# Low halves of the weights all on VectorE, the first norm's affine in half tiles, and new step lengths around the layer-B softmax

## The chip, the cores and the metric

The program runs on one core of a Trainium2 chip. The metric is the device time of one execution in microseconds, from the first instruction to the last. The time shown is the median of three executions. A profile is one more execution, recorded on the chip, with a time of its own.

## The reference, cut to what matters

Two blocks run one after the other, each on 256 tokens (two tiles of 128). The first is a pooling mixer (layer A), a layer norm, and a mixer with dilated window attention (layer B); the second is two attention layers with their MLPs (layer0, mlp0, layer1, mlp1). The change touches the first norm and layer B's attention directly, and the weights of layer B's end, layer0, mlp0's first part and layer1.

```python
def layer_norm(x, g, b):
    mu = jnp.mean(xf, axis=-1, keepdims=True)
    var = jnp.mean(jnp.square(xf - mu), axis=-1, keepdims=True)
    y = (xf - mu) * lax.rsqrt(var + LN_EPS) * g + b
...
for l in range(DEPTH):
    if l < N_A_LAYERS: y = pool_mixer(h, ...)        # layer A
    else:              y = dilated_mixer(h, w_in_b, w_out_b, k_sh, v_sh, slopes)  # layer B
    h = layer_norm(DN_ALPHA * h + y, ln_g[l], ln_b[l])
    if l == N_A_LAYERS - 1:
        kv = h @ w_kv          # keys and values of layer B
...
# dilated_window_attention, per head and dilation:
scores = jnp.einsum('bnqrhd,bnkrhd->bnrhqk', qb, kk) * (HEAD_DIM ** -0.5)
p = jnp.exp(scores + bias - lse[..., None])
out = jnp.einsum('bnrhqk,bnkrhd->bnqrhd', p, vv)
```

All of it is float32. Every product with a weight matrix `h @ w` is the bulk of the work.

## The kernel before, in words

**Products.** A float32 product is made of three reduced-precision ones (`mm3`): high part by high part (L189), high by low (L190), low by high (L191), all summed in PSUM. So each weight block is loaded by `stream` as a tile `ws` of 128x1024, ScalarE (ACT) casts it to the high part `wh` (L130), and the low part `wl = ws - wh` is made either by VectorE (DVE) in one instruction of 128x1024 (L138) or by GpSimd (POOL) in two of 128x512 (L136). The string `self.lo` decides: its letters are walked through load by load, D is DVE and P is POOL. It is "D" in layers A and B and "DP" or "DDP" in stretches of layer0, mlp0 and layer1, so that 31 of 336 loads go to POOL. There are five buffers each of `wh` and `wl`. Activations are split in the same way (`split`: L143 on ACT, L144 on DVE).

**Order.** TensorE (PE) runs its instructions in the order in which the code is written. The work of the side generators is woven into the projections: `tick(us)` advances a clock by the estimated length of the projection step just written, adds `us * ratio` to a budget, and calls `step` until the budget is spent; each `yield x` of a generator takes x from it. The other engines are ordered by a scheduler, which also takes `issue_after(i)` (it keeps an instruction behind i) and `high_priority` into account. Every engine then runs its own list in order and waits for semaphores of the others.

**The first norm.** `out_norm` calls `layer_norm` for each tile t of tokens: sum with the residual (L548) and statistics (L549) on DVE, `rstd`, whose power runs on POOL (L177, priority raised), normalization on DVE (L557, two halves of 512 columns), then the affine n*g+b with rows of g and b that are broadcast to all partitions (L498, POOL, 128x1024, a product and a sum for each tile). The transposed copy that feeds layer B doesn't need the affine in that form: `norm_T` transposes n on PE (L385) and applies g and b per partition while evacuating PSUM (L410 on DVE), then splits into high and low (L143, L144). The L498 result is used as residual after layer B.

**Attention of layer B.** `attn1` is one generator for each of eight head pairs, woven into the projections of the following head pair. For each of two query tiles (qt) it makes scores for two heads on PE (L668), adds the distance bias (L672, DVE), takes the row maximum (L673, DVE) and the exponential (L674, ACT), and yields. Then 1/sum (L678) and the scaling (L680) on DVE, four groups of transposes of the weights on PE (L690, evacuated by L691), and products with the values (L703). L276 are small PE products for a modulation vector, put between.

**Norms of the second block** follow the same pattern: L1075 and L1078 (residual with gate), L174 and L177 (rstd), L720 (normalization), L385 (transposes). L750, L756 and L758 are the rotary embedding (L756 on POOL).

Of the kernel before, what the change touches and what calls it, by code (L numbers as in the profile page):

```python
# [8 lines left out]
F32 = mybir.dt.float32  # L9
F32R = mybir.dt.float32r  # L10
AF = mybir.ActivationFunctionType
ALU = mybir.AluOpType
# [51 lines left out]
class Kern:  # L64
    def __init__(self, tc, I, out):
        self.tc, self.nc, self.I, self.out = tc, tc.nc, I, out
        self.clock = 0.0
        self.due = []
        self.sides = []
        self.budget = 0.0  # L70
        self.ratio = 0.0
        self.marks = set()
        self.mupto = 99
        self.nload = 0
        self.lo = "D"
# [47 lines left out]
    def stream(self, src):  # L123
        nc = self.nc
        k, c = src.shape[1], src.shape[2]
        n = k * c
        ws = self.wp.tile([128, 1024], F32, name="ws", tag="ws", bufs=4)
        nc.sync.dma_start(ws[:, :n].rearrange("p (k c) -> p k c", k=k), src)
        wh = self.wp.tile([128, 1024], F32R, name="wh", tag="wh", bufs=5)
        nc.scalar.copy(wh[:, :n], ws[:, :n])  # L130
        wl = self.wp.tile([128, 1024], F32R, name="wl", tag="wl", bufs=5)
        self.nload += 1
        if self.lo[self.nload % len(self.lo)] == "P":
            for i in range(0, n, 512):
                c = slice(i, i + 512)
                nc.gpsimd.tensor_tensor(wl[:, c], ws[:, c], wh[:, c].bitcast(F32), op=ALU.subtract)  # L136
        else:
            nc.vector.tensor_sub(wl[:, :n], ws[:, :n], wh[:, :n].bitcast(F32))  # L138
        return (wh[:, :n].rearrange("p (k c) -> p k c", k=k),
                wl[:, :n].rearrange("p (k c) -> p k c", k=k))  # L140
# [291 lines left out]
    def layer_a(self):  # L432
        nc, I = self.nc, self.I
# [10 lines left out]
        with self.tc.tile_pool(name="pa", bufs=1) as pa:  # L444
# [9 lines left out]
            n = 0  # L454
# [40 lines left out]
        with self.tc.issue_after(pw.ins):  # L495
            for n in ns:
                for z, op in ((self.lng[0], ALU.mult), (self.lng[1], ALU.add)):
                    nc.gpsimd.tensor_tensor(n, n, z, op=op)  # L498
# [81 lines left out]
    def layer_b(self):  # L580
# [5 lines left out]
        for cb in range(6):  # L586
# [18 lines left out]
            if cb == 3:  # L605
                with self.tc.issue_after(i0.ins), self.tc.issue_after(i1.ins):
                    self.tables()
        wq = I["w_in_b"][0]
        mg = self.fms(4, F32)
        with self.tc.tile_pool(name="pb", bufs=2) as pb:  # L610
# [3 lines left out]
            for hp in range(8):  # L614
# [20 lines left out]
                self.weave(self.attn1(hp, kq[1], kq[0], vt, mg[hp // 2][:, (hp % 2) * 256:(hp % 2) * 256 + 256]), 0.58)  # L635
# [18 lines left out]
    def attn1(self, hp, q, k, vt, mg):  # L654

        nc = self.nc
        sbs = [self.pb.tile([128, 2, 512], F32, name="sb") for _ in range(2)]
        st = [[self.sm(2) for _ in range(3)] for _ in range(2)]
        for qt in range(2):
# [15 lines left out]
            yield 2.0  # L675
# [5 lines left out]
        yield 0.8  # L681
        pts = []
        for r in range(2):
            pt = [self.fm(F32) for _ in range(2)]
            for i in range(2):
                ps = self.ps("B")
                for b in range(2):
                    for qt in range(2):
                        c, d = (i * 2 + b) * 128, (b * 2 + qt) * 128
                        nc.tensor.transpose(ps[:, d:d + 128], sbs[r][:, qt, c:c + 128], self.ident)  # L690
                (nc.scalar.copy if i else nc.vector.tensor_copy)(pt[i], ps)  # L691
                yield 0.5
            pts.append([pt[i // 2][:, (i % 2) * 256:(i % 2) * 256 + 256] for i in range(4)])
            yield 1.2
# [5 lines left out]
        for n, (g, b, kt, Q) in enumerate(todo):  # L700
# [4 lines left out]
            if n % 2:  # L705
                yield 0.8
# [397 lines left out]
    def layer0(self):  # L1104
        nc, I = self.nc, self.I
        self.X[1] = [(x[:, 0:512], x[:, 512:1024]) for x in self.xt]
        self.lo = "DP"
# [68 lines left out]
        self.lo = "DP"  # L1176
        self.in_block(0, acts, 0, 512, (0, 1), fin_qa)
        self.lo = "D"
# [17 lines left out]
        self.lo = "DP"  # L1196
        wv = self.in_block(0, acts, 1792, 512, (0,), fin_vb)
        self.lo = "DDP"
# [6 lines left out]
        self.lo = "DDP"  # L1205
        self.out_cols(0, osl, 0, fill)
        self.lo = "DP"
# [55 lines left out]
    def mlp0(self):  # L1263
        nc, I = self.nc, self.I
        joint = self.j1
        self.lo = "DP"
# [8 lines left out]
        for c in range(4):  # L1275
            hh, hl = self.hidden(0, c, act, 512, first if c == 0 else None)
            if c == 0:
                self.lo = "D"
# [65 lines left out]
    def mlp1(self):  # L1344
        nc, I = self.nc, self.I
        act = self.act1
        self.lo = "D"
# [51 lines left out]
    def layer1(self):  # L1399
        nc, I = self.nc, self.I  # L1400
        acts = {s: self.act256(*self.hs1[s]) for s in (0, 1)}
        self.lo = "DP"
# [154 lines left out]
```

## Time and profile before

| what | value |
|---|---|
| time, median of 3 (lowest, highest) | 1553.2 us (1547.85, 1554.77) |
| profiled execution, its own time | 1556.21 us |
| span of the profile | 1554.4 us |
| busy PE, DVE, ACT, POOL | 1481.7, 920.0, 722.8, 248.7 us |
| mean granted clock of PE | 0.983 |

The span is 1.8 us shorter than the profiled execution's time, and this execution lies 3 us above the median. An engine that is busy for 95% of the span can only be made to end earlier by closing its gaps or by letting it run at full clock; the rows below list gaps with the engine and instruction that ended them.

### The profile page before, as it was taken

How to read it: one execution, taken by the hardware profiler on the slowest of the kernel's cores; microseconds unless marked ns; L12 is line 12 of the kernel's file. 1: busy time of each engine (PE TensorE's matmuls, PEld its weight loads, DVE VectorE, ACT ScalarE, POOL GpSimd, SP SyncE). 2: the span in 40 equal slices, each digit the busy share in tenths (PEclk: the TensorE clock that was granted, in tenths of full speed). 3: DMA queues.
4: the chain of work that ended last, by engine and by line, in shares of the span. 5: the costliest groups of instructions: out<-in, count | busy, mean ns of one | idle time of the engine just before them, and what ended most of it. 6: DMA issues, size and time to landing. Idle time of an engine off the chain costs nothing. (4 is left out here: it accounts for less than half of the span.)

```text
span 1554.4 us, 23369 instructions
## 1 busy us (share of the span) xinstructions
PE 1481.7 (95%) x8966; PEld 1224.9 (79%) x8966; DVE 920.0 (59%) x1629; ACT 722.8 (46%) x1397; POOL 248.7 (16%) x298
## 2 busy tenths in 40 slices
PE   8999899999999899999879999999998999999998
PEld 8898578887999687776668777777886886689987
DVE  5676855556667867457685233343448687565554
ACT  4454444444455545556564232231326476454443
POOL 4431200001010342113330000000014423100000
PEclk9999899999999999999999999999999999999999
DMA  8567576766464723013333444443353345645652
GB/s 279 188 195 262 166 225 184 230 188 211 130 199 150 245 94 94 30 55 122 120 110 120 151 149 136 149 137 121 95 161 97 109 97 202 229 138 190 189 183 89
DMA packets 186544, 241.80 MB, mean 156 GB/s; under 512 B 15296, under 2 KB 132080, under 8 KB 186368
## 3 DMA queue, kind: packets, MB, share of 16 engines
q1 hardware_dynamic: 185168, 237.11, 48.2%
q0 software_dynamic: 1264, 3.19, 0.6%
q8 instruction: 70, 1.15, 0.3%
q14 instruction: 42, 0.34, 0.1%
HBM read 239.19 MB, written 2.03 MB: 155 GB/s over the span
## 5 line engine op out<-in xcount | busy, mean ns | idle before, releaser
L138 DVE TENSOR_TENSOR wl<-ws,wh 128x1024 fp32r<-128x1024 f32 x305 | 377.9, 1240 | 360.3 <-ACT wh L130 351.0
L130 ACT CAST wh<-ws 128x1024 fp32r<-128x1024 f32 x336 | 351.0, 1048 | 401.3 <-PE ps L191 205.6
L189 PE MATMUL ps<-fm,wh 128*128 128x256 f32 (+1 forms) x1416 | 432.8, 306 | 4.5 <-ACT fm L143 4.4
L191 PE MATMUL ps<-fm,wl 128*128 128x256 f32 (+1 forms) x1416 | 426.0, 301 | 7.5 <-DVE wl L138 7.5
L190 PE MATMUL ps<-fm,wh 128*128 128x256 f32 (+1 forms) x1416 | 425.4, 300 | 0.3 <-DVE fm L144 0.3
L189 PE MATMUL ps<-wh,fm 128*128 128x512 f32 (+1 forms) x912 | 364.7, 400 | 0.0
L190 PE MATMUL ps<-wl,fm 128*128 128x512 f32 (+1 forms) x912 | 356.0, 390 | 6.3 <-DVE wl L138 6.3
L191 PE MATMUL ps<-wh,fm 128*128 128x512 f32 (+1 forms) x912 | 356.1, 390 | 2.7 <-DVE fm L144 2.7
L189 PEld LDWEIGHTS ps<-fm,wh 128*128 128x128 f32 x1416 | 271.5, 192 | 30.0 <-issue 7.1
L191 PEld LDWEIGHTS ps<-fm,wl 128*128 128x128 f32 x1416 | 271.8, 192 | 18.4 <-DVE wl L138 9.2
L190 PEld LDWEIGHTS ps<-fm,wh 128*128 128x128 f32 x1416 | 272.2, 192 | 9.6 <-DVE fm L144 0.7
L189 PEld LDWEIGHTS ps<-wh,fm 128*128 128x128 f32 x912 | 173.4, 190 | 58.4 <-issue 18.5
L191 PEld LDWEIGHTS ps<-wh,fm 128*128 128x128 f32 x912 | 172.9, 190 | 43.7 <-DVE fm L144 5.2
L190 PEld LDWEIGHTS ps<-wl,fm 128*128 128x128 f32 x912 | 173.5, 190 | 42.9 <-DVE wl L138 8.1
L136 POOL TENSOR_TENSOR wl<-ws,wh 128x512 fp32r<-128x512 f32 x62 | 87.9, 1437 | 498.3 <-ACT wh L130 444.1
L143 ACT CAST fm<-t 128x128 fp32r<-128x128 f32 (+2 forms) x232 | 85.0, 393 | 137.7 <-POOL t L474 51.5
L144 DVE TENSOR_TENSOR fm<-t,fm 128x128 fp32r<-128x128 f32 (+2 forms) x232 | 95.0, 434 | 57.8 <-ACT fm L143 56.8
L177 POOL TENSOR_TENSOR sm<-sm,mhalf 128x1 f32<-128x1 f32 (+3 forms) x42 | 37.2, 885 | 393.7 <-DVE sm L174 298.2
L926 ACT ACTIVATE e<-ps,sm 128x512 f32<-128x512 f32 (+1 forms) x96 | 59.3, 618 | 50.0 <-DVE sm L922 34.8
L922 DVE TENSOR_REDUCE sm<-ps 128x1 f32<-128x512 f32 (+1 forms) x96 | 56.1, 589 | 12.8 <-PE ps L1041 9.2
L870 POOL CAST fm<-fm 64x256 fp32r<-64x256 f32 x32 | 18.0, 563 | 231.0 <-ACT fm L867 218.2
L1340 DVE SCALAR_TENSOR_TENSOR t<-ps,t 128x512 f32<-128x512 f32 (+1 forms) x64 | 35.4, 552 | 18.5 <-ACT t L1339 18.5
(204 smaller groups left out, 1287.6 us busy)
## 6 DMA issues: line engine op xcount, KB each, us to landing
ws<-in_w_mlp_in_dram SPq DMA_DIRECT2D x64, 512.0 KB, 3.8
ws<-in_w_mlp_out_dram SPq DMA_DIRECT2D x64, 512.0 KB, 3.8
mw<-in_w_mod_dram SPq DMA_DIRECT2D x48, 512.0 KB, 4.9
fm<-in_w_mod_dram SPq DMA_DIRECT2D x96, 256.0 KB, 5.4
ws<-in_w_kv_dram SPq DMA_DIRECT2D x48, 512.0 KB, 3.9
ws<-in_w_in_dram SPq DMA_DIRECT2D x40, 512.0 KB, 4.0
ws<-in_w_in_a_dram SPq DMA_DIRECT2D x32, 512.0 KB, 5.0
ws<-in_w_in_b_dram SPq DMA_DIRECT2D x32, 512.0 KB, 4.0
```

The costliest lines, as they stand in the source:

```text
L130: nc.scalar.copy(wh[:, :n], ws[:, :n])
L136: nc.gpsimd.tensor_tensor(wl[:, c], ws[:, c], wh[:, c].bitcast(F32), op=ALU.subtract)
L138: nc.vector.tensor_sub(wl[:, :n], ws[:, :n], wh[:, :n].bitcast(F32))
L143: self.nc.scalar.copy(hi, src)
L144: self.nc.vector.tensor_sub(lo, src, hi.bitcast(F32))
L177: self.pow = nc.gpsimd.tensor_tensor(r, v, self.mhalf[:, :n], op=ALU.pow)
L189: nc.tensor.matmul(ps, a[0], b[0], start=start, stop=False)
L190: nc.tensor.matmul(ps, a[0], b[1], start=False, stop=False)
L191: nc.tensor.matmul(ps, a[1], b[0], start=False, stop=stop)
L922: nc.vector.tensor_reduce(nm, ps[:, :n], axis=AX.X, op=ALU.max, negate=True)
L926: nc.scalar.activation(e, ps[:, :n], AF.Exp, bias=nm, accum_out=ss)
L1340: nc.vector.scalar_tensor_tensor(q, p, 0.0, r, op0=ALU.max, op1=ALU.mult)
```

## The change

The low parts made by POOL are made by DVE; the pattern string, its counter and the L136 branch are gone. The affine of the first norm leaves `out_norm`; it becomes a list of eight half-tile instructions, of which two each are issued after the evacuation of a value block (cb = 1 to 4) in layer B, with `issue_after` on that block's two evacuations. In `attn1` the ratio goes from 0.58 to 0.66 and the lengths of the yields change.

```diff
@@ stream
-        self.nload += 1
-        if self.lo[self.nload % len(self.lo)] == "P":
-            for i in range(0, n, 512):
-                c = slice(i, i + 512)
-                nc.gpsimd.tensor_tensor(wl[:, c], ws[:, c], wh[:, c].bitcast(F32), op=ALU.subtract)
-        else:
-            nc.vector.tensor_sub(wl[:, :n], ws[:, :n], wh[:, :n].bitcast(F32))
+        nc.vector.tensor_sub(wl[:, :n], ws[:, :n], wh[:, :n].bitcast(F32))
@@ end of layer A
-        with self.tc.issue_after(pw.ins):
-            for n in ns:
-                for z, op in ((self.lng[0], ALU.mult), (self.lng[1], ALU.add)):
-                    nc.gpsimd.tensor_tensor(n, n, z, op=op)
+        self.affine = [(n[:, c:c + 512], z[:, c:c + 512], op) for n in ns for c in (0, 512)
+                       for z, op in ((self.lng[0], ALU.mult), (self.lng[1], ALU.add))]
@@ layer_b, after i0 and i1 of value block cb
+            if cb:
+                with self.tc.issue_after(i0.ins), self.tc.issue_after(i1.ins):
+                    for _ in range(2):
+                        if self.affine:
+                            n, z, op = self.affine.pop(0)
+                            nc.gpsimd.tensor_tensor(n, n, z, op=op)
@@ attn1
-                self.weave(self.attn1(hp, kq[1], kq[0], vt, mg[hp // 2][:, (hp % 2) * 256:(hp % 2) * 256 + 256]), 0.58)
+                self.weave(self.attn1(hp, kq[1], kq[0], vt, mg[hp // 2][:, (hp % 2) * 256:(hp % 2) * 256 + 256]), 0.66)
-            yield 2.0
+            yield (1.5, 3.2)[qt]
...
-        yield 0.8
+        yield 1.2
...
-                yield 0.5
+                yield 0.4
...
-            yield 1.2
+            yield 0.6
...
-                yield 0.8
+                yield 0.6
@@ layer0, the first of the lines that set self.lo
-        self.lo = "DP"
...
```

Three places show how the instructions stand before and after. In the program after, lines have other numbers: L138 of before is L130, L144 is L136, L177 is L169, L498 is L604, L668 is L665, L690 is L687, L276 is L268, L189 is L181, L174 is L166, L720 is L717, L1075 and L1078 are L1072 and L1075.

POOL, from the end of layer A into layer B, before:

```order
70 L613 DMA dist<-in_dist_dram 128x1024
71 L177 TENSOR_TENSOR sm<-sm,mhalf 128x1 x2
72 L498 TENSOR_TENSOR xt<-xt,gb 128x1024 x4
73 L804 TENSOR_TENSOR t_2547<-t_2545 128x128
74 L870 COPY fm<-fm 64x256 x24
```

and after:

```order
70 L610 DMA dist<-in_dist_dram 128x1024
71 L169 TENSOR_TENSOR sm<-sm,mhalf 128x1
72 L604 TENSOR_TENSOR xt<-xt,gb 128x512 x4
73 L169 TENSOR_TENSOR sm<-sm,mhalf 128x1
74 L604 TENSOR_TENSOR xt<-xt,gb 128x512 x4
75 L801 TENSOR_TENSOR t_2547<-t_2545 128x128
```

The first tile's four affine instructions stand ahead of the power (L169) of the second tile's rstd, where before both powers stood ahead of all of them; `issue_after` names instructions of DVE and ACT, and in POOL's list no instruction of layer B stands ahead of them.

PE, head pair 1 of layer B, before (three matmuls L189, L190, L191 repeat eight times in each gap of 24 rows, shown as "..."; a gap of 48 rows holds sixteen such threes):

```order
1775 L668 MATMUL ps<-fm 128x128 x4
...
1801 L668 MATMUL ps<-fm 128x128 x4
1802 L276 MATMUL ps<-mw,S 32x512 x4
...
1827 L690 MATMUL ps<-ident,sb 128x128 x4
...
1852 L690 MATMUL ps<-ident,sb 128x128 x4
1853 L276 MATMUL ps<-mw,S 32x512 x4
1854 L690 MATMUL ps<-ident,sb 128x128 x4
...
1879 L690 MATMUL ps<-ident,sb 128x128 x4
```

and after:

```order
1774 L665 MATMUL ps<-fm 128x128 x4
1775 L874 MATMUL ps<-fm 128x256 x4
1776 L665 MATMUL ps<-fm 128x128 x4
...
1801 L268 MATMUL ps<-mw,S 32x512 x4
...
1850 L687 MATMUL ps<-ident,sb 128x128 x12
1851 L268 MATMUL ps<-mw,S 32x512 x4
1852 L687 MATMUL ps<-ident,sb 128x128 x4
```

The scores of both query tiles now stand back to back. Between the last scores and the first transposes lay one group of 24 matmuls and an L276; now there are three groups and an L268, and the transposes follow one another where a group of 24 stood between them.

DVE, the first norm of mlp0 (xt is a token tile, t_8584 and t_8576 its normalized form), before:

```order
827 L174 TENSOR_SCALAR sm<-sm 128x1
828 L1078 SCALAR_TENSOR_TENSOR xt<-t_8571,sm,xt 128x512
829 L1078 SCALAR_TENSOR_TENSOR xt<-t_8572,sm,xt 128x512
830 L138 TENSOR_TENSOR wl<-ws,wh 128x1024
831 L174 TENSOR_SCALAR sm<-sm 128x1
832 L720 TENSOR_SCALAR t_8584<-xt,sm 128x512 x2
```

and after:

```order
844 L166 TENSOR_SCALAR sm<-sm 128x1
845 L130 TENSOR_TENSOR wl<-ws,wh 128x1024
846 L1075 SCALAR_TENSOR_TENSOR xt<-t_8563,sm,xt 128x512
847 L1075 SCALAR_TENSOR_TENSOR xt<-t_8564,sm,xt 128x512
848 L130 TENSOR_TENSOR wl<-ws,wh 128x1024 x2
849 L166 TENSOR_SCALAR sm<-sm 128x1
850 L130 TENSOR_TENSOR wl<-ws,wh 128x1024
851 L717 TENSOR_SCALAR t_8576<-xt,sm 128x512 x2
```

Four low parts (L130) stand between the first L166 and the normalization (L717), where one (L138) stood.

## Rows read from the trace of the kernel before

**Rows 1.** Page, part 1: busy time, share of the span and instructions of each engine.
```profile
PE 1481.7 (95%) x8966; PEld 1224.9 (79%) x8966; DVE 920.0 (59%) x1629; ACT 722.8 (46%) x1397; POOL 248.7 (16%) x298
```

**Rows 2.** Waits of PE: total us, times, longest.
```profile
PE ps L385 <- DVE t L720: 12.5, 6, 4.1
...
PE ps L690 <- DVE sb L680: 6.2, 4, 1.9
```

**Rows 3.** Windows (columns us, busy us of each engine, granted clock, DMA share, GB/s).
```profile
302.30:305.70 3.40, 3.40 (x19) 3.40 (x18) 2.51 (x5) 0.00 (x0) 0.00 (x0) 0.51 0.77 226
...
391.00:394.40 3.40, 3.40 (x18) 3.40 (x18) 1.47 (x3) 0.00 (x0) 0.00 (x0) 0.52 0.70 199
...
1234.10:1237.50 3.40, 3.40 (x18) 3.30 (x17) 0.68 (x2) 0.83 (x2) 0.00 (x0) 0.52 0.36 128
```

**Rows 4.** Groups by line: busy us, mean ns of one, idle before.
```profile
L138 DVE TENSOR_TENSOR wl<-ws,wh 128x1024 fp32r<-128x1024 f32 x305 | 377.9, 1240 | 360.3 <-ACT wh L130 351.0 <-DMA fm<-in_w_mod_dram 5.6 <-PE ps L703 1.9
...
L136 POOL TENSOR_TENSOR wl<-ws,wh 128x512 fp32r<-128x512 f32 x62 | 87.9, 1437 | 498.3 <-ACT wh L130 444.1 <-DVE sm L924 24.9 <-issue 14.6
...
L672 DVE SCALAR_TENSOR_TENSOR sb<-dist,ps 128x512 f32<-128x512 f32 x32 | 20.6, 683 | 4.4 <-PE ps L668 4.1
...
L673 DVE TENSOR_REDUCE sm<-sb 128x1 f32<-128x512 f32 x32 | 20.9, 677 | 0.0
...
L680 DVE TENSOR_SCALAR sb<-sb,sm 128x512 f32<-128x512 f32 x32 | 14.2, 483 | 0.2
```

**Rows 5.** Timeline, first head pair: start, us, engine, line.
```profile
294.56 0.71 PE L668 MATMUL ps<-fm 64*128 64x128 f32 x8
...
296.19 0.39 PE L189 MATMUL ps<-fm,wh 128*128 128x256 f32 x1
...
300.65 0.88 DVE L680 TENSOR_SCALAR sb<-sb,sm 128x512 f32<-128x512 f32 x2
...
301.24 0.90 PE L690 MATMUL ps<-ident,sb 128*128 128x128 f32 x4 [1.95 <-issue]
```

**Rows 6.** Timeline, first norm into layer B.
```profile
176.37 1.00 DVE L557 TENSOR_SCALAR xt<-t,sm 128x512 f32<-128x512 f32 x2 [0.69 <-POOL sm L177]
...
182.70 4.83 POOL L498 TENSOR_TENSOR xt<-xt,gb 128x1024 f32<-128x1024 f32 x2
...
182.77 5.04 DVE L557 TENSOR_SCALAR xt<-t,sm 128x512 f32<-128x512 f32 x2 [0.35 <-POOL sm L177]
...
194.34 0.79 PE L191 MATMUL ps<-wh,fm 128*128 128x512 f32 x1 [2.33 <-DVE fm L144]
```

**Rows 7.** Timeline, out projection of layer0 and start of mlp0.
```profile
778.24 0.88 DVE L720 TENSOR_SCALAR t<-fm,sm 128x512 f32<-128x512 f32 x2 [0.33 <-POOL sm L177]
...
778.78 1.09 PE L385 MATMUL ps<-ident,t 128*128 128x128 f32 x8 [2.53 <-DVE t L720]
...
781.31 2.69 POOL L136 TENSOR_TENSOR wl<-ws,wh 128x512 fp32r<-128x512 f32 x2
...
781.38 2.91 DVE L720 TENSOR_SCALAR t<-fm,sm 128x512 f32<-128x512 f32 x2 [0.33 <-POOL sm L177]
...
798.18 0.38 PE L191 MATMUL ps<-fm,wl 128*128 128x256 f32 x1 [2.35 <-DVE wl L138]
...
808.87 1.97 PE L385 MATMUL ps<-ident,t 128*128 128x128 f32 x8 [4.13 <-DVE t L720]
```

**Rows 8.** Timeline, five other places where PE waits near a POOL load.
```profile
534.99 0.38 PE L190 MATMUL ps<-wl,fm 128*128 128x256 f32 x1 [1.20 <-DVE wl L138]
...
631.12 1.94 PE L961 MATMUL ps<-pt,fm 128*64 128x256 f32 x14 [2.60 <-ACT pt L945]
...
755.34 1.17 PE L1014 MATMUL ps<-fm,t 128*128 128x128 f32 x8 [2.61 <-ACT t L945]
...
1189.63 0.62 PE L190 MATMUL ps<-wl,fm 128*128 128x512 f32 x1 [3.37 <-DVE wl L138]
...
1232.92 1.49 PE L847 MATMUL ps<-identr,t 128*128 128x128 f32 x15 [3.07 <-DVE t L144]
```

More of the change, by code (lines that the diff above doesn't have):

```diff
@@ L73, in __init__ @@
         self.mupto = 99
-        self.nload = 0
-        self.lo = "D"
     def defer(self, delay, fn):
@@ L1175, in layer0 @@
             self.defer(d, lambda: self.more(1))
-        self.lo = "DP"
         self.in_block(0, acts, 0, 512, (0, 1), fin_qa)
-        self.lo = "D"
         o = {}
@@ L1195, in layer0 @@
         self.in_block(0, acts, 1280, 512, (0, 1), fin_b(kb, None))
-        self.lo = "DP"
         wv = self.in_block(0, acts, 1792, 512, (0,), fin_vb)
-        self.lo = "DDP"
         self.weave(self.attn_diff((0, 1), qb, kb, vb, osl, 2), 1.2)
@@ L1204, in fill @@
             self.need_side(("o", 0) if k >= 4 else ("a", len(js) - 1))
-        self.lo = "DDP"
         self.out_cols(0, osl, 0, fill)
-        self.lo = "DP"
         self.j1 = self.joint_slots()
@@ L1265, in mlp0 @@
         joint = self.j1
-        self.lo = "DP"
         ctx, x = slice(0, 256), slice(256, 512)
@@ L1277, in mlp0 @@
             if c == 0:
-                self.lo = "D"
                 self.mupto = 35
@@ L1346, in mlp1 @@
         act = self.act1
-        self.lo = "D"
         for f in self.xT:
@@ L1401, in layer1 @@
         acts = {s: self.act256(*self.hs1[s]) for s in (0, 1)}
-        self.lo = "DP"
         for d in (1.0, 2.5, 4.0, 7.0, 9.0):
```

## The prediction

> **What bounds the kernel now.** I read the page first: PE is busy for 1481.7 of 1554.4 us and DVE for 920.0 [rows 1]. So PE sets the end, and the change can only give what PE loses in gaps (1554.4 - 1481.7 = 72.7 us) and in stretches at half clock. Then the waits of PE: its longest entry is for the normalizations L720, 12.5 us in six waits, and the scaled softmax L680 costs 6.2 us in four [rows 2]. Last, windows on the granted clock: behind some waits there are 3.4 us at 0.51, which is the lower of the two levels (1.2 and 2.4 GHz), while PE is busy throughout [rows 3]. Such a stretch costs about half its length, 1.7 us. The reader is to see that no engine beside PE is full on average; what counts is which instruction is late at each gap.
>
> **Attention.** Before, the last scores of head pair 0 end at T = 295.3 (294.56 + 0.71) and PE comes to the first transposes after one group of 24 matmuls (296.19 to 299.29, so about 3.0 us with its start) and an L276. The scaled weights (L680, 300.65) aren't there, and L690 starts at 301.24 after 1.95 us of waiting [rows 5]. With the three long ones of the four waits on L680 (longest 1.9, sum 6.2, so the fourth is about 0.6) [rows 2] this makes 8.2 us. Three of the four long waits are followed by a stretch at 0.51; the first and the last are shown [rows 3]. That is 3 x 1.7 = 5.1 us more.
>
> After, three groups and an L268 lie between: 3 x 2.9 + 0.5 = 9.2 us from T. But the order puts both query tiles' scores back to back, so DVE must do both softmaxes in one go: four L672 of 0.683, four L673 of 0.677 [rows 4], of which about 1.3 lies before T, so they end at T + 4.1; then the splits and rotations that the order shows between (about 1.3), two reciprocals, one low part of 1.24 which waits for its cast, two L680 of 0.483 [rows 4]. I put the first head's weights at T + 8.6 and, behind one more low part, the second's at T + 10.8. PE wants the first at T + 9.2, which is met, and the second one after eight transposes of the first, at T + 10.2: a new wait of about 0.6 to 0.7, in the four head pairs 0 to 3 (from pair 4 on, the order has a group of 24 between the two heads' transposes, and PE reaches the first 0.5 sooner, so 0.2 is left at most). Added: about 3. Net: -8.2 - 5.1 + 3 = -10. Ends: -4 if the half-clock stretches stay or only move, -13 if nothing waits.
>
> **The affine in half tiles.** The order shows that it isn't done in layer B. POOL runs the first tile's four halves as soon as PE has transposed that tile, ahead of the power of the second tile's rstd. What that does is read from the rows: with POOL idle, two L557 take 1.00 us; beside L498 the same two take 5.04 [rows 6]. A half tile on POOL is put at half of L498 (4.83 for two, so 1.2 each) [rows 6]. So four of them, from about 180.2, end at 185.1; the second rstd is late by 3 us (L557 started at 182.77) and then normalizes in 1.0 instead of 5.04. It ends at about 186.8 instead of 187.8. The second tile's four halves then meet the splits L144, which end this stage before at 194.34 behind a 2.33 us wait [rows 6]; four alternating blocks of 1.2 hold up four splits instead of two blocks of 2.4 holding up two. I take +1. Ends: -3 (splits slip through), +4 (the rstd's delay comes through whole).
>
> The Trainium skill (SBUF — State Buffer, section SBUF: two separate sides) says that GpSimd and a VectorE instruction with two SBUF inputs take the shared port pair as an exclusive lock for a whole instruction. The trace agrees for the pair of L557 beside L498, which is 5 times as long, although L557 reads one tile only. By the page alone shorter POOL instructions would hold the lock more briefly and the half tiles would be worth something; by the rows the sum of POOL's work is the same and only the order of turns changes. With the page's reading the term would be about -1 (a split waits at most 1.2 instead of 2.4), with mine it is +1.
>
> **Low parts on DVE.** Removed: 62 POOL instructions of 1.437 us, 87.9 us in all. Added: 31 instructions of 1.240 on DVE, 38 us [rows 4]. On average DVE has room (920.0 + 38 of 1554) [rows 1]. It is worth something only where PE waits, so place by place:
> - Out projection and first norm of mlp0 (768 to 811). PE waits 2.53 at 778.78, 2.35 at 798.18, 4.13 at 808.87 [rows 7], about 10 with two small ones. A pair of L720 takes 0.88 alone and 2.91 beside POOL's L136 [rows 7]. By the same measure the pairs of L1078 and the low parts there lose another 6, so DVE loses some 8 to POOL; the four loads that come to DVE here add 5.0. The four low parts that stand ahead of the normalization (order) cost 3 x 1.24 more there, of which about 3 is won back by unstretched neighbours and cover for the power. DVE gets 3 ahead, and the powers no longer queue behind POOL's halves. I take -5; ends -1 and -8.
> - Before layer0 PE waits 1.20 at 534.99 for a DVE low part that runs beside POOL's [rows 8]: -1.0.
> - At 631.12 (2.60) and 755.34 (2.61) the late engine is ACT, whose input comes from DVE and the rotary work that waited for POOL's L136 [rows 8]: -1.3 and -1.4, half of each.
> - At 1232.92 PE waits 3.07 for a split, behind rotary work (L756) that had queued on POOL behind L136 [rows 8]: -3.0; the half-clock stretch at 1234.1 [rows 3] goes with it, -1.7.
> - At 1189.63 PE waits 3.37 for a low part of DVE itself [rows 8]; one more ahead of it costs 0.7 net of POOL's disturbance: +0.7.
> - Elsewhere in layer0 and layer1 loads run ahead by up to five buffers, and the cover for a late low part is that lead; without it each load is 1.24 on PE. I take 0.
> Sum: -5 - 1.0 - 1.3 - 1.4 - 3.0 - 1.7 + 0.7 = -12.7. Ends: -18, and for loss, 0.
>
> **Sum.** -10 + 1 - 12.7 = -21.7 against the profiled execution's 1556.2: 1534.5. The median lies 3.0 below that execution, so in its terms 1531.5. I forecast 1532.
>
> **The rivals.**
> 1. The low parts are neutral: what DVE wins by not being stretched it pays with 31 x 1.24. For it: 38 us added is more than all the waits in rows 7 and 8 together. Against it: L720 is three times as long beside L136 [rows 7], and the split wait at 1232.92 has nothing to do with DVE's load. Result: -10 + 1 = -9, so 1544.
> 2. The two softmaxes in one go give the attention back. Decisive is when the second head's weights come: if at T + 12.5 or later, PE waits 2.3 in four pairs (9.2) and the half-clock stretches remain. That is 9.2 - 8.2 = 1 to the bad, so with the low parts' -12.7 and the affine's +1, -10.7: 1543. Against it: no instruction in the order would take these 2 us more on DVE, except a low part that waits for ACT's cast behind the exponentials.
> 3. Slower: DVE becomes the bound in layer0 and layer1. In the order, low parts stand ahead of normalizations and splits on which PE waits. Each that PE sees costs 1.24 [rows 4]; the gain of -9 elsewhere is used up by 8 of 31, and slower by over 0.5% of 1553.2 (7.8 us, about what a measurement of this kernel can tell from no change) needs 14. With all 31 it is 1553.2 - 9 + 38 = 1582. Against it: the five-buffer lead, and PE's waits on low parts before are short.
> 4. The halves do run in layer B, as the code reads, and not where the order puts them (my forecast is that there the change doesn't do what it says). For it: only the code's place. Then the 4.0 us of stretched L557 [rows 6] and about 4 of held-up splits come back instead of the +1, 9 us more than I count: 1523.
>
> The Trainium skill (Perfetto Trace Analysis, section Optimizing Scalar/DVE Operations) allows offloading a saturated VectorE to GpSimd but warns that between these two it might not help because they share a read port. Its first half speaks for rival 3, its second for my sum. This trace agrees with the warning [rows 7]; DVE is at 59% of the span, so the first half's condition isn't met on average.
>
> **How the numbers follow.** My forecast with its own spread (1522 to 1541, from the ends of its terms, which don't all fall on one side): 0.58. Rival 1: 0.17. Rival 2: 0.12. Rival 3: 0.08. Rival 4: 0.05. The range 1519 to 1547 takes in rivals 1, 2 and 4 (1544, 1543, 1523) with some spread and leaves out rival 3 and the tails. Faster by over 0.5% means under 1545.4: all of the forecast and rival 4, six in ten of rivals 1 and 2, in all 0.80; within 0.5% 0.14, the rest of these and the start of rival 3; slower 0.06, rival 3 from 14 loads on.
>
> **What would show it.** Attention right: no wait of about 1.9 at the transposes, at most about 0.7 at the second head's, clock at 1.00 through 300 to 395. Wrong: PE's wait on the scaling above 6 us in total. Affine: POOL's four halves at about 180 to 185, the second power near 185, first product of layer B near 195. Low parts right: L720 pairs at about 0.88, L1078 pairs at 1.4, PE's wait on L720 clearly below 12.5 in total, DVE's busy time between 920 and 958 because stretching goes. Wrong: PE waits for a low part longer than the 3.37 us that is its longest here [rows 8], or DVE is busy without a gap from 770 to 800. What would make the whole prediction wrong is a place where DVE's new load delays a split or a normalization that was early before, which no wait of before can show.

## The result and the profile after

The changed kernel takes 1526.0 us (median of four, 1525.73 to 1527.2), the kernel before 1551.02 us (median of four by then). The ratio is 0.9839 with a 95% interval of 0.9813 to 0.9866: 25 us faster. The profiled execution is 1525.75 us, 30.5 under that of before (1556.21). That one lay high: 2.8 us of the difference were already there after PE's first 1152 matmuls, before any edit acts. So 27.7 us between the traces stand for 25.0 between the medians. Of the 30.4 us between the two spans (1554.4 and 1524.0), 17.9 are gaps of PE (72.7 before, 54.8 after) and 12.5 its busy time. The program asks the same 8966 matmuls of PE in both; the mean granted clock rose from 0.983 to 0.990, which taken over the spans is an estimate of at most 11 us (0.017 of 1554.4 is 26, 0.010 of 1524.0 is 15).

The page's first part, as in [rows 1]:

```profile
PE 1469.2 (96%) x8966; PEld 1213.7 (80%) x8966; DVE 924.6 (61%) x1660; ACT 721.2 (47%) x1397; POOL 172.8 (11%) x240
```

POOL lost 75.9 us. DVE got 31 more low parts of 1.23, which is 38 us, but is busy only 4.6 us longer than before. So some 33 us of DVE's busy time before are gone; about 30 of them go with the low parts alone (experiment below). They were not work but DVE's instructions taking longer beside POOL's. The groups show examples (busy, mean ns of one, idle before). Before:

```profile
L1078 DVE SCALAR_TENSOR_TENSOR xt<-t,sm,xt 128x512 f32<-128x512 f32 x16 | 14.5, 942 | 4.9 <-POOL sm L177 4.9
...
L720 DVE TENSOR_SCALAR t<-xt,sm 128x512 f32<-128x512 f32 x16 | 8.1, 549 | 4.4 <-POOL sm L177 4.2
```

and after:

```profile
L130 DVE TENSOR_TENSOR wl<-ws,wh 128x1024 fp32r<-128x1024 f32 x336 | 413.7, 1233 | 357.5 <-ACT wh L128 347.2 <-DMA fm<-in_w_mod_dram 5.6 <-PE ps L700 3.3
...
L1075 DVE SCALAR_TENSOR_TENSOR xt<-t,sm,xt 128x512 f32<-128x512 f32 x16 | 11.4, 747 | 4.3 <-POOL sm L169 4.3
L604 POOL TENSOR_TENSOR xt<-xt,gb 128x512 f32<-128x512 f32 x8 | 11.2, 1425 | 5.4 <-PE ps L377 5.4
...
L717 DVE TENSOR_SCALAR t<-xt,sm 128x512 f32<-128x512 f32 x16 | 7.1, 484 | 3.7 <-POOL sm L169 3.6
```

L717 (L720 before) takes 0.484 on average now, 0.549 before; beside POOL one of a pair took half of 2.91 [rows 7]. L1075 (L1078 before) takes 0.747 where it took 0.942. A half tile of the affine (L604) takes 1.425 on POOL, where 1.2 was put.

Waits of PE (us in total, times, longest), answering to [rows 2]. For the low parts before:

```profile
PE ps L191 <- DVE wl L138: 7.5, 8, 2.3
...
PE ps L190 <- DVE wl L138: 6.3, 5, 3.4
```

and after:

```profile
PE ps L182 <- DVE wl L130: 10.5, 8, 2.9
...
PE ps L377 <- DVE t L717: 5.7, 4, 3.2
...
PE ps L183 <- DVE wl L130: 4.9, 6, 1.6
```

The wait for normalizations fell from 12.5 to 5.7, the one for the scaled softmax is gone altogether (no line on L687), and the waits for low parts are 15.4 in their two lines, where they were 13.8. The windows on the granted clock (columns as in [rows 3]) show a norm stage that is at half clock only in part, where before it was so throughout, and the whole attention at full clock. Before:

```profile
186.20:199.90 13.70, 9.34 (x24) 4.43 (x25) 13.70 (x24) 4.63 (x15) 6.78 (x4) 0.51 0.37 115
```

and after:

```profile
186.20:199.90 13.70, 10.96 (x37) 6.71 (x30) 11.44 (x17) 4.29 (x15) 4.62 (x4) 0.76 0.69 218
260.00:440.00 180.00, 179.20 (x1534) 157.72 (x1534) 114.01 (x181) 89.95 (x167) 16.86 (x29) 1.00 0.71 212
```

To set stages side by side I count PE's matmuls, of which each program here has 8966, nearly all in the same order, and take the time between the starts of two numbers in each trace (us). "Attn", "low" and "half" are the kernels with one edit alone, "7 back" and "DVE" two further experiments below.

```
matmul no.    before  after  attn   low    half  7 back  DVE    what
0    - 1152   170.2  167.4  167.4  167.9  168.0  168.4  167.9   layer A, no edit acts
1152 - 1408    66.5   65.2   67.2   67.0   64.9   65.1   58.7   norm into layer B
1536 - 3456   238.8  223.9  223.7  237.1  237.0  223.6  225.1   layer B's attention
3968 - 4224    48.3   45.0   49.8   45.0   49.8   49.8   45.0   layer0, rotary embedding near 625
4608 - 4736    25.5   27.3   25.5   27.3   25.5   27.3   27.3   layer0, out projection
4736 - 5120    76.7   67.5   74.1   67.7   74.1   75.7   68.9   norms, start of mlp0
6656 - 6784    30.8   32.1   30.8   32.2   30.8   30.1   30.1   start of layer1
6784 - 7040    40.6   37.4   40.6   37.5   40.6   38.0   37.4   layer1, rotary embedding near 1228
7040 - 7680    97.1   98.4   97.1   98.2   97.1   98.1   98.1   layer1's attention
```

Two of the columns without the low parts' edit differ from before at 3968 (49.8 against 48.3) and 4736 (74.1 against 76.7), although their programs are the same there. Half-clock stretches fall at other moments from one execution to the next; differences of 1 to 3 us of a single trace are read with that in mind. The start of layer1 shows it best: it takes 30.1 us in the two traces without such a stretch there, 30.8 with 3.4 us of it (before) and 32.1 with 6.8 us (after).

### The profile page after: what moved, and what is told of

Its sections match the earlier page's. It is cut to its first block, busy times and chain, and to the rows that moved or that the text cites. A ratio compares the mean times of both kernels' runs of the same rounds, so it can differ in the third digit from the quotient of the medians.

```text
span 1524.0 us, 23366 instructions
## 1 busy us (share of the span) xinstructions
PE 1469.2 (96%) x8966; PEld 1213.7 (80%) x8966; DVE 924.6 (61%) x1660; ACT 721.2 (47%) x1397; POOL 172.8 (11%) x240
## 3 DMA queue, kind: packets, MB, share of 16 engines
q8 instruction: 70, 1.15, 0.3%
## 4 chain that ended last, share of the span: by engine, by line
PE 68%; DVE 9%; POOL 4%; ACT 3%; issue 3%; DMA 1%; SPq 0%; POOLq 0%; DVEq 0%; ACTq 0%
PE ps L181 20%; PE ps L182 19%; PE ps L183 19%; POOL sm L169 2%; DVE wl L130 2%; PE ps L958 2%; PE ps L874 2%; PE ps L268 2%; PE ps L940 1%; PE ps L700 1%; PE ps L687 1%; POOL t L753 1%; DVE fm L136 1%; DVE sm L919 1%; PE ps L665 1%
## 5 line engine op out<-in xcount | busy, mean ns | idle before, releaser
L130 DVE TENSOR_TENSOR wl<-ws,wh 128x1024 fp32r<-128x1024 f32 x336 | 413.7, 1233 | 357.5 <-ACT wh L128 347.2
L181 PE MATMUL ps<-fm,wh 128*128 128x256 f32 (+1 forms) x1416 | 428.2, 302 | 4.2 <-ACT fm L135 4.2
L181 PE MATMUL ps<-wh,fm 128*128 128x512 f32 (+1 forms) x912 | 364.0, 399 | 0.3 <-ACT fm L135 0.3
L181 PEld LDWEIGHTS ps<-fm,wh 128*128 128x128 f32 x1416 | 267.7, 189 | 30.5 <-issue 10.9
L183 PEld LDWEIGHTS ps<-fm,wl 128*128 128x128 f32 x1416 | 267.7, 189 | 15.6 <-DVE wl L130 6.7
L182 PEld LDWEIGHTS ps<-fm,wh 128*128 128x128 f32 x1416 | 267.6, 189 | 9.8 <-DVE fm L136 0.7
L181 PEld LDWEIGHTS ps<-wh,fm 128*128 128x128 f32 x912 | 172.4, 189 | 58.7 <-issue 17.7
L182 PEld LDWEIGHTS ps<-wl,fm 128*128 128x128 f32 x912 | 172.8, 189 | 48.3 <-DVE wl L130 14.0
L135 ACT CAST fm<-t 128x128 fp32r<-128x128 f32 (+2 forms) x232 | 85.5, 394 | 133.6 <-POOL t L466 50.8
L169 POOL TENSOR_TENSOR sm<-sm,mhalf 128x1 f32<-128x1 f32 (+3 forms) x42 | 39.4, 938 | 872.4 <-DVE sm L166 696.2
L136 DVE TENSOR_TENSOR fm<-t,fm 128x128 fp32r<-128x128 f32 (+2 forms) x232 | 90.2, 410 | 55.9 <-ACT fm L135 55.0
L1327 ACT ACTIVATE t<-ps 128x512 f32<-128x512 f32 (+1 forms) x64 | 31.2, 487 | 31.9 <-PE ps L183 31.9
L940 PE MATMUL ps<-ident,e 128*128 128x128 f32 x272 | 42.1, 274 | 2.6 <-ACT e L923 1.1
```

The lines of the kernel that those rows point to most:

```text
L135: self.nc.scalar.copy(hi, src)
L136: self.nc.vector.tensor_sub(lo, src, hi.bitcast(F32))
L169: self.pow = nc.gpsimd.tensor_tensor(r, v, self.mhalf[:, :n], op=ALU.pow)
L181: nc.tensor.matmul(ps, a[0], b[0], start=start, stop=False)
L182: nc.tensor.matmul(ps, a[0], b[1], start=False, stop=False)
L183: nc.tensor.matmul(ps, a[1], b[0], start=False, stop=stop)
```

## The experiments

Every ratio is to runs of the kernel before on the same chip. The experiments ran on four chips, on which the kernel before took 1551.9 to 1553.7 us, so a distance to the change's 1526.0 by the medians can be off by some 2 us; where it matters, the distance by the ratios stands beside it.

**One edit alone.** The kernel before with the new steps of `attn1`:

```diff
-                self.weave(self.attn1(hp, kq[1], kq[0], vt, mg[hp // 2][:, (hp % 2) * 256:(hp % 2) * 256 + 256]), 0.58)
+                self.weave(self.attn1(hp, kq[1], kq[0], vt, mg[hp // 2][:, (hp % 2) * 256:(hp % 2) * 256 + 256]), 0.66)
-            yield 2.0
+            yield (1.5, 3.2)[qt]
...
```

> The kernel before with the new steps of attn1 alone (ratio and yields). Theory A (the three edits act at separate places and add up; in layer B's attention PE loses four waits of about 1.9 us and three stretches at half clock, 13 us, and gets no new wait): 12 to 15 us under before, no wait of PE on the scaled softmax over 0.3 us, granted clock 1.0 from 260 to 440 us. Rival B (the low parts or the affine share in the gain seen there): 4 to 8 us under before, with half-clock stretches left between 300 and 400 us.

Measured: 1538.88 us, ratio 0.9915 (0.990 to 0.993), 13 us faster. The wait on L680 is gone from the trace, and the attention takes 223.7 instead of 238.8. Theory A holds; the other two edits have no share in these waits (with either of them alone, PE waits 6.2 us in four there, as before).

The kernel before with all low parts on DVE:

```diff
-        if self.lo[self.nload % len(self.lo)] == "P":
...
-        else:
-            nc.vector.tensor_sub(wl[:, :n], ws[:, :n], wh[:, :n].bitcast(F32))
+        nc.vector.tensor_sub(wl[:, :n], ws[:, :n], wh[:, :n].bitcast(F32))
```

> The kernel before with all low parts on DVE alone. Theory A: 9 to 13 us under before; the attention keeps its four waits of about 1.9 us on the scaled softmax and its half-clock stretches, the stretch from 768 to 811 us is 6 to 9 us shorter, and near 1180 us it loses 1 to 2 us. Rival C (low parts neutral, as 38 us land on DVE): within 3 us of before.

Measured: 1540.17 us, ratio 0.9921 (0.9907 to 0.9936), 12 us faster. The attention keeps its waits (6.2 us in four). Theory A holds, in the stage and in the total. The page of this run has DVE's busy time with this edit alone:

```profile
PE 1477.7 (96%) x8966; PEld 1218.0 (79%) x8966; DVE 928.4 (60%) x1660; ACT 721.9 (47%) x1397; POOL 171.0 (11%) x236
```

That is 8.4 us more than before for 38 us of added work.

The kernel before with the half tiles:

```diff
-        with self.tc.issue_after(pw.ins):
-            for n in ns:
-                for z, op in ((self.lng[0], ALU.mult), (self.lng[1], ALU.add)):
-                    nc.gpsimd.tensor_tensor(n, n, z, op=op)
+        self.affine = [(n[:, c:c + 512], z[:, c:c + 512], op) for n in ns for c in (0, 512)
+                       for z, op in ((self.lng[0], ALU.mult), (self.lng[1], ALU.add))]
...
+                            nc.gpsimd.tensor_tensor(n, n, z, op=op)
```

> The kernel before with the affine in half tiles alone. Theory A: within 2 us of before, since the half tiles still run on POOL beside the norm; the second power is 3 us late and the normalization after it takes 1.0 instead of 5.0 us. Rival D (shorter POOL instructions let DVE through, so the norm's stage is shorter and its half-clock stretch too): 3 to 6 us under before.

Measured: 1552.14 us in ten runs against 1552.03, ratio 1.000 (0.999 to 1.0011). Theory A holds: nothing. The three edits alone give -13.1, -11.9 and +0.1, together -24.9, and the change gives -25.0. They add up, as far as an interval of 4 us to either side of the change's ratio can tell.

**More on POOL.** The pattern "P" wherever it was "DP" or "DDP", which makes 64 loads' low parts on POOL instead of 31.

```diff
-        self.lo = "DP"
+        self.lo = "P"
...
```

> The kernel before with the pattern P wherever it was DP or DDP, so that about twice as many low parts run on POOL. Theory A (POOL's instructions take turns with DVE's and stand ahead of POOL's powers): 6 to 14 us over before, with L720 and L1078 stretched at more places. Rival C: between 4 us under and 3 us over before, since DVE is relieved of another 38 us.

Measured: 1569.1 us, ratio 1.011 (1.0093 to 1.0127), 17 us slower, more than theory A's 14. PE's waits name the same places, only longer (12.5 and 3.8 before):

```profile
PE ps L385 <- DVE t L720: 17.0, 5, 5.8
PE ps L847 <- DVE t L144: 7.0, 2, 6.3
```

These two are longer by 7.7 us; the mean granted clock is 0.977 instead of 0.983, some 9 us by the estimate above. Relieving DVE of another 33 low parts, 41 us of its work, made the program slower, and DVE's busy time fell by only 16.9 us (to 903.1). Rival C falls on both sides.

**What the steps of the attention do.** The second yield at 2.2: two groups of 24 matmuls before the transposes instead of three.

```diff
-            yield (1.5, 3.2)[qt]
+            yield (1.5, 2.2)[qt]
```

> The changed kernel with the second yield after the scores at 2.2 instead of 3.2, so that the scores stay back to back but two groups instead of three stand before the transposes. Theory A (what counts is that PE comes later than DVE's weights, which are ready 8.9 us after the last scores): PE comes at about 6.7 us and waits about 2.2 us in head pairs 0 to 3, so 8 to 9 us of waits on L677, with half-clock stretches behind some of them: 1534 to 1540 us. Rival E (only the number of waits between engines or the ratio matters): within 2 us of the changed kernel, 1526.

Measured: 1543.79 us, ratio 0.9953 (0.9938 to 0.9968), 18 us slower than the changed kernel. The direction is theory A's, the size is beyond it (1534 to 1540). Rival E falls. The group of the transposes (L687, after the last | the idle time before) shows 11.2 us of waiting, where the changed kernel has 0.0:

```profile
L687 PE MATMUL ps<-ident,sb 128*128 128x128 f32 x128 | 18.7, 278 | 11.2 <-DVE sb L677 9.4 <-issue 1.5
```

Four waits of 1.7 to 1.8 us by start-to-start distance in head pairs 0 to 3 are what was expected; two more of 2.8, in later pairs, were not. Of 17.2 us in the attention these waits are 11.2 and one half-clock stretch 1.7; the other 4 were not taken apart.

The first yield at 2.4: the scores apart again, and two groups and L268 behind the last.

```diff
-            yield (1.5, 3.2)[qt]
+            yield (2.4, 3.2)[qt]
```

> The changed kernel with the first yield at 2.4 instead of 1.5, so that a group of 24 stands between the scores of the two query tiles again, and two groups plus L268 between the last scores and the transposes. Theory A: the second softmax alone needs about 6.2 us as before the change, PE comes at about 6.7 us, so no wait over 0.5 us: within 2 us of the changed kernel's 1526. Rival F (back-to-back scores are what gave the gain): 5 us or more slower.

Measured: 1531.31 us, ratio 0.9868 (0.9854 to 0.9883): about 5 us slower than the change (5.3 by the medians, 4.5 by the ratios), 20.6 faster than before. One wait of 0.6 on L677 is left, where theory A allowed 0.5, and the attention takes 226.6 (223.9 changed, 238.8 before). So most of the gain needs no back-to-back scores; but it isn't within 2 us. The profiled execution lies 6.8 us over that of the change: 2.7 of it are in the attention, 2.3 in layer A, where no edit acts and a half-clock stretch fell in this trace, and 1.4 at the norms of mlp0, where the programs are the same. Theory A misses its number; rival F's 5 us are met by the medians and not by the ratios. In the attention itself, back-to-back scores are worth at most some 3 us.

**Where the affine belongs.** The same eight half tiles on DVE, where `issue_after` names an instruction of the same engine and does hold them in layer B.

```diff
-                            nc.gpsimd.tensor_tensor(n, n, z, op=op)
+                            nc.vector.tensor_tensor(n, n, z, op=op)
```

> The changed kernel with the eight half-tile instructions on DVE, where the order does hold them behind the evacuations of layer B. Theory A (POOL's part at the norm is what costs: powers late, splits held up): the second normalization starts 2.3 us sooner, the splits run at 0.3 us each, the stage from 172 to 206 us gets 4 to 8 us shorter, 1518 to 1522 us. Rival G (the stage is set by the chain statistics, power, transposes, and the half clock): within 2 us of 1526.

Measured: 1520.99 us, ratio 0.9804 (0.9788 to 0.982), 5 us under the change, inside theory A's 1518 to 1522. The timeline of the changed kernel at the norm (as in [rows 6]):

```profile
173.74 1.00 DVE L548 TENSOR_SCALAR xt<-t,sm 128x512 f32<-128x512 f32 x2 [0.69 <-POOL sm L169]
...
177.28 5.15 POOL L604 TENSOR_TENSOR xt<-xt,gb 128x512 f32<-128x512 f32 x4 [3.58 <-PE ps L377]
...
182.39 0.55 POOL L169 TENSOR_TENSOR sm<-sm,mhalf 128x1 f32<-128x1 f32 x1
182.98 1.00 DVE L548 TENSOR_SCALAR xt<-t,sm 128x512 f32<-128x512 f32 x2 [2.53 <-POOL sm L169]
...
183.58 1.97 PE L377 MATMUL ps<-ident,xt 128*128 128x128 f32 x8 [3.24 <-DVE xt L548]
...
184.78 6.04 POOL L604 TENSOR_TENSOR xt<-xt,gb 128x512 f32<-128x512 f32 x4 [1.83 <-PE ps L377]
...
192.26 0.49 PE L183 MATMUL ps<-wh,fm 128*128 128x512 f32 x1 [2.47 <-DVE fm L136]
```

and with the affine on DVE in layer B:

```profile
179.81 0.55 POOL L169 TENSOR_TENSOR sm<-sm,mhalf 128x1 f32<-128x1 f32 x1 [5.84 <-DVE sm L164]
180.40 1.00 DVE L548 TENSOR_SCALAR xt<-t,sm 128x512 f32<-128x512 f32 x2 [0.35 <-POOL sm L169]
...
181.00 1.11 PE L377 MATMUL ps<-ident,xt 128*128 128x128 f32 x8 [0.39 <-DVE xt L548]
...
186.50 0.50 PE L183 MATMUL ps<-wh,fm 128*128 128x512 f32 x1 [0.43 <-DVE fm L136]
```

In the first, the four halves of one tile end at 182.4 and the power that DVE needs runs only then; in the second it runs at 179.8, and PE waits 0.39 and 0.43 where it waited 3.24 and 2.47. From 172 to 210 us the granted clock is 0.87 in the first and 1.00 in the second; this stage (matmuls 1152 to 1408) takes 58.7 instead of 65.2 us, and 58.7 again in the two later kernels that have the affine on DVE. The row of the window with the affine on DVE:

```profile
172.00:210.00 38.00, 35.11 (x169) 24.62 (x168) 28.05 (x52) 19.55 (x37) 1.97 (x3) 1.00 0.54 170
```

The half tiles on POOL behind both powers:

```diff
+        self.pw = pw
...
-                with self.tc.issue_after(i0.ins), self.tc.issue_after(i1.ins):
+                with self.tc.issue_after(self.pw.ins):
```

> The changed kernel with the half tiles on POOL behind both powers, as whole tiles stood before. Theory A: the second power is 2.4 us sooner, the normalization after it takes turns with the half tiles and takes 3.4 to 5 instead of 1.0 us; both even out, within 2 us of 1526. Rival H (the late power is a cost of its own): 2 to 4 us faster, 1522 to 1524.

Measured: 1528.06 us, ratio 0.9853 (0.9838 to 0.9867), 2.1 us over the change by the medians and 2.2 by the ratios, the stage 65.9 against 65.2. Rival H falls. Theory A has the size about right, but what evens out is not what it named (L605 and L549 are L604 and L548 of the change):

```profile
179.59 0.55 POOL L169 TENSOR_TENSOR sm<-sm,mhalf 128x1 f32<-128x1 f32 x1 [5.84 <-DVE sm L164]
180.11 10.96 POOL L605 TENSOR_TENSOR xt<-xt,gb 128x512 f32<-128x512 f32 x8
180.18 2.89 DVE L549 TENSOR_SCALAR xt<-t,sm 128x512 f32<-128x512 f32 x2 [0.35 <-POOL sm L169]
...
182.99 6.95 DVE L136 TENSOR_TENSOR fm<-t,fm 128x128 fp32r<-128x128 f32 x5
...
191.30 0.80 PE L181 MATMUL ps<-wh,fm 128*128 128x512 f32 x1 [6.02 <-ACT fm L135]
```

The power is 2.8 us sooner and the normalization takes 2.89, so it still ends 0.9 sooner than the change's (183.07 against 183.98). The loss comes behind it: the eight half tiles stand in one row until 191.07, five splits (L136) beside them take 6.95 us where the first five of the change take 1.60, and PE waits 6.02.

**Which low parts matter.** Eight of the 31 back on POOL, chosen from the places that the prediction named:

```diff
...
-        nc.vector.tensor_sub(wl[:, :n], ws[:, :n], wh[:, :n].bitcast(F32))
+        self.nload += 1
+        if self.nload in (161, 170, 171, 173, 175, 177, 251, 253):
+            for i in range(0, n, 512):
+                c = slice(i, i + 512)
+                nc.gpsimd.tensor_tensor(wl[:, c], ws[:, c], wh[:, c].bitcast(F32), op=ALU.subtract)
+        else:
+            nc.vector.tensor_sub(wl[:, :n], ws[:, :n], wh[:, :n].bitcast(F32))
```

> The changed kernel with 8 of the 31 low parts back on POOL, those beside a rotary embedding (two places) and beside the normalizations and powers from 740 to 811 us. Theory A (these few places made the gain of 12 us): 8 to 12 us over 1526, so 1534 to 1538. Rival J (each of 31 is worth 0.4): 3 us over, 1529.

Measured: 1528.94 us; ratio 0.9837 (0.9823 to 0.9851), the same as the change's 0.9839, though by the medians 2.9 us over it. Theory A's number fell; rival J's 1529 is met by the medians and not by the ratios, so this run doesn't settle it. Only two of these eight, by their start times in the trace before, ran at the places meant (746 and 771 us); the others ran at 664, 729, 736, 761, 1201 and 1214 us. The two at 729 and 736 stand at the out projection, which won 0.9 us (26.4 instead of 27.3). So the places that were meant were left to be tried:

```diff
...
+        if self.nload in (159, 173, 177, 179, 181, 183, 255):
...
```

> The changed kernel with 7 of the 31 low parts back on POOL, now those that ran on POOL at 622, 746, 771, 781, 794, 799 and 1223 us of the kernel before: right ahead of a rotary embedding on POOL (two) and among the powers and normalizations (five). Only two of these seven (746 and 771) were among the eight loads of the run before. Theory A (these places made the gain): 620 to 646 us loses 3, 740 to 822 us loses 5 to 9, 1204 to 1236 us loses 3: 9 to 13 us over 1526, 1535 to 1539. Rival J (each POOL low part is worth 0.4): 3 us over, 1529.

Measured: 1535.15 us, ratio 0.9884 (0.9868 to 0.9901): 9.2 us over the change by the medians, 7.0 by the ratios (0.0045 of 1552). Rival J's 1529 falls: seven of 31 carry more than half of the 12 us. By stage, in a trace that is the slowest of the four executions (1538.37): 4.8 at the rotary embedding near 625, 8.2 at the norms from 746 to 823, but only 0.6 near 1228, where theory A had 3; there it takes more than the one load. And the start of layer1 won 2.0 us in this trace with no edit near: no half-clock stretch fell there. PE's wait for normalizations is up again, from 5.7 to 7.1 (L384 and L724 are L377 and L717 here):

```profile
PE ps L384 <- DVE t L724: 7.1, 4, 2.6
```

That is the smaller part of the 8.2. All waits of PE at these norms together are 3.4 us longer than the change's (10.8 and 7.4), and the granted clock there is 0.91 instead of 0.97, some 5 us by the estimate above. The windows, of the changed kernel and of this one (columns as in [rows 3]):

```profile
730.20:797.70 67.50, 60.07 (x386) 53.11 (x386) 49.56 (x113) 41.98 (x108) 7.48 (x9) 0.97 0.39 118
...
736.10:811.80 75.70, 64.89 (x387) 57.79 (x385) 54.75 (x110) 42.10 (x108) 18.64 (x17) 0.91 0.34 109
```

The other way round: the affine on DVE, and low parts back on POOL where the kernel with all of them on DVE lost against before. First:

```diff
...
+        if self.nload in (164, 167, 243, 245, 257, 259, 261, 263):
...
```

> The kernel with the affine on DVE, and eight low parts back on POOL, chosen where the traces show PE waiting for a low part of DVE or a loss against before when all are on DVE: two of the output projection of layer0 (near 725 us), two and four of layer1's input (near 1165 and 1250 to 1310 us). Theory A (the price of a low part depends on its place): the 1.8, 1.4 and 1.0 us that all on DVE lost there come back, 3 to 4 us under the 1521 of the affine on DVE, 1516 to 1519. Rival J (any POOL low part costs about 0.4 us, 12 over 31): 3 us over it, 1524.

Measured: 1519.93 us, ratio 0.978 (0.9766 to 0.9793), 1.1 us under the affine on DVE by the medians and 3.7 by the ratios. Rival J's 1524 falls; theory A's 1516 to 1519 is missed by the median, and of the three losses that were to come back only the out projection's did, 0.9 of 1.8: layer1's attention stayed at 98.0, and the start of layer1 took 31.6 with 6.8 us of half clock. The norms won 1.4, with no edit there and a half-clock stretch fewer. It lost 1.6 near 1228. There load 257 (L135) runs right behind the last embedding, not ahead of it as the expectation of the next run has it, and beside the DVE instruction that adds the embedding's products (L762):

```profile
1188.12 3.25 POOL L760 TENSOR_TENSOR t<-t,rope 128x128 f32<-128x128 f32 x4 [3.85 <-ACT t L1408]
1191.33 2.97 POOL L135 TENSOR_TENSOR wl<-ws,wh 128x512 fp32r<-128x512 f32 x2
1191.40 1.76 DVE L762 TENSOR_TENSOR t<-t,t 128x512 f32<-128x512 f32 x1 [1.20 <-POOL t L760]
...
1194.90 1.90 PE L851 MATMUL ps<-identr,t 128*128 128x128 f32 x15 [1.88 <-DVE t L143]
```

The instruction takes 1.76 here and 0.69 in the same trace at 1184.31, where POOL is idle. PE's wait behind it is 1.88 instead of the change's 1.49; the rest of the 1.6 is a half-clock stretch of 3.4 us from 1195.4 on, which the change does not have there. Then without 257, with 170 and 171:

```diff
...
+        if self.nload in (164, 167, 170, 171, 243, 245, 259, 261, 263):
...
```

> The kernel with the affine on DVE and nine low parts on POOL: four of layer0's output projection, two of layer1's input at its start and three after its rotary embeddings (the load ahead of an embedding that cost 1.8 us at 1204 to 1236 us in the mixed run is back on DVE). Theory A: 1.8 us under the mixed run's 1519.9 there and up to 1 us near 725 us, so 1516.5 to 1518.5. Rival K (what is won at one place is lost to another wait behind it): within 1 us of 1520.

Measured: 1517.31 us, ratio 0.9771 (0.9756 to 0.9785): the fastest here, 8.7 us under the change. The out projection is back at 25.5 and the stage near 1228 at 37.3, so theory A's number (1516.5 to 1518.5) holds, with the neighbour corrected as above, and rival K falls. Layer1's attention stays at 98.0: putting three low parts back on POOL there won nothing.

## Why the prediction was right

The forecast was 1532 (1519 to 1547), the time is 1526.0; -21.7 was summed and -25.0 measured.

*Attention, -10 summed, -13.1 alone.* The mechanism is as it was put; the mis-sized term is the added wait. "the second one after eight transposes of the first, at T + 10.2: a new wait of about 0.6 to 0.7 [...] Added: about 3" didn't happen. The rows of the changed kernel, with the last scores ending at T = 288.06:

```profile
287.35 0.71 PE L665 MATMUL ps<-fm 64*128 64x128 f32 x8
...
296.04 0.88 DVE L677 TENSOR_SCALAR sb<-sb,sm 128x512 f32<-128x512 f32 x2
...
297.78 1.73 PE L687 MATMUL ps<-ident,sb 128*128 128x128 f32 x12
298.04 0.87 DVE L677 TENSOR_SCALAR sb<-sb,sm 128x512 f32<-128x512 f32 x2
```

The weights are ready at T + 8.9 and T + 10.9 (forecast 8.6 and 10.8), but PE comes at T + 9.7, not 9.2, and eight transposes take 1.15 (8/12 of 1.73), so it wants the second head at T + 10.9, just when it is there. The lead misses by nothing; one group less and PE waits 11.2 us. Without this term the sum is -13.3, which is what the run gave. Rival 2 (the softmax in one go gives the attention back) falls: it needed T + 12.5.

*Affine, +1 summed, 0 measured.* The power is late by what the order showed (182.39, where 185 was forecast; this execution was some 2.6 us ahead there, so it is 185 on the clock of before), the normalization takes 1.00, and both even out. Rival 4's price was tested on DVE only: with the halves really in layer B the kernel gains 5 us (6.5 in the stage), not 9. The Trainium skill (SBUF — State Buffer, section SBUF: two separate sides) has the lock held for a whole instruction, so that shorter POOL instructions should let DVE in sooner. The trace with the half tiles behind both powers agrees: the normalizing pair takes 2.89 beside them and took 5.04 beside whole tiles [rows 6]. By that reading the prediction had put the term at -1. The stages bear it out rather than the +1: matmuls 1152 to 1408 take 64.9 to 65.9 us in the seven traces with half tiles on POOL, and 66.5 to 67.2 in the four with whole ones. The medians of the half tiles alone, 1.000 (0.999 to 1.0011), show no gain and would allow one of up to 1.5 us.

*Low parts, -12.7 summed, -11.9 alone.* The sum is right, its places are partly wrong, and that they cancel is luck: by the traces before and after, 4.8 us more came at two places than was counted and 5.9 less at the others. The norms gave 9.2 where 6.4 were counted from 746 to 823 (against the two kernels without the low parts' edit, only 6.6). Near 625 3.3 came where 1.3 was counted: the wait of 2.60 went whole and not by half. Near 1228 it was 3.2 where 4.7 was counted. The start of layer1 lost 1.3, 0.7 was counted, and that is a longer half-clock stretch (6.8 us instead of 3.4); ahead of layer0 0.3 came of the 1.0 (95.5 after 95.8), and nothing with this edit alone (95.9). Not counted at all were two places that lose: 1.8 at the out projection and 1.3 in layer1's attention. PE waits there for no low part, but for ACT's exponentials and DVE's work on the attention heads: 1.5 instead of 0.7 and 2.7 instead of 1.7 in total, which is 0.8 of the 1.8 and 1.0 of the 1.3. The longest wait of each after:

```profile
705.25 0.66 PE L940 MATMUL ps<-ident,e 128*128 128x128 f32 x4 [0.51 <-ACT e L923]
...
1282.09 0.96 PE L1454 MATMUL ps<-fm 64*128 64x512 f32 x5 [0.95 <-ACT e L923]
```

Before, neither of these two waited. That DVE comes later to its part of the softmax, with more low parts in its list, is a likely reason and was not followed further. "DVE's busy time between 920 and 958" held at 924.6, and that it is so near the lower end is the answer to rival 1 and rival 3: the 31 low parts took DVE 38 us and gave it back some 30 (the other 3 to 4 go with the affine, whose normalizing pair takes 1.00 instead of 5.04).

The Trainium skill (Perfetto Trace Analysis, section Optimizing Scalar/DVE Operations) warns that moving work between VectorE and GpSimd might not help because of the shared port. The runs agree and go further: with 33 low parts more on POOL the time rose by 17 us, with 31 fewer it fell by 12.

## What to carry to other kernels

Read an engine's busy time together with its neighbour's: DVE at 59% looked free to take 38 us, and it was, because some 30 us of that 59% were instructions that took longer beside POOL's and went with them. For a side generator that is woven into a busy engine, count from the moment its input ends to the moment the slow engine's answer is ready, and put at least that much work between; here one group of 24 matmuls, about 2.9 us, decided over some 18 us. Look at the engine's own list before trusting an ordering hint: here one that named instructions of other engines left POOL's half tiles (L604) at 177 us, ahead of layer B, while with the same hint on DVE, which runs one of the named instructions, they ran from 209.7 us on.

## What was not expected

The half clock carries a good part of what the edits gain, up to 11 us of the 30.4 between the traces beside 17.9 of gaps. With the affine on DVE the stage from 172 to 210 us runs at 1.00 instead of 0.87, and PE's waits there shrank from 3.24 and 2.47 to 0.39 and 0.43; the two can't be told apart by these runs. In the attention of the kernel before, three of four waits of 1.9 us were followed by 3.4 us at 0.51, one was not; with two groups before the transposes, six waits of 1.7 to 2.8 us (start to start) were followed by one such stretch. So a wait doesn't always bring the lower clock, and what decides is left open.

The order of the products costs PE something, too. With the scores apart, PE waits only 0.6 us for the weights, and yet the attention takes 2.7 us more. From start to start of PE's products, 2.1 us of it lie between one value product (L700) and the next, 1.1 at changes from one kind of product to another (127 instead of 119), and the rest gives 0.5 back. Why the value products take longer there wasn't tried.
